# Expert weights in stored blocks of 16 KB per partition, in a ring of ten 16 KB slots and one of 8 KB

## The chip, the cores and the metric

The kernel runs on one core of one Trainium2 chip. The metric is the device time of the program in microseconds (us): three runs of the kernel before took 1932.21, 1930.95 and 1932.10 us, the median is 1932.1 us. All data are f32; weights come from HBM (the chip's main memory) into SBUF (128 partitions of on-chip memory), matrix products go to PSUM.

## What is computed

One layer of a diffusion backbone: a state-space branch and an attention branch over 512 latent tokens, then a routed feed-forward part. The change touches only the last part:

```python
def expert_choice_ffn(h, w_router, w_gate, w_up, w_down):
    cap = CAPACITY_FACTOR * n // N_EXPERTS            # 2 * 512 // 16 = 64 tokens for each of 16 experts
    aff = softmax(h @ w_router)
    gate, idx = top_k(aff.T, cap)
    xs = h[bidx, idx]
    hid = silu(einsum('becd,edf->becf', xs, w_gate)) * einsum('becd,edf->becf', xs, w_up)
    ys = einsum('becf,efd->becd', hid, w_down) * gate[..., None]
    return zeros_like(h).at[bidx, idx].add(ys)
# w_gate, w_up: 16 x 1024 x 2816, w_down: 16 x 2816 x 1024, f32
```

So each of 16 experts reads three matrices of 1024 x 2816 f32, 11 MiB each: 33 MiB an expert, 528 MiB (553.6 MB) in all. Every byte is read once.

## The kernel before

Everything up to about 610 us of the span is the two branches, the output projection and the router; the expert loop follows. `gather(e)` collects the 64 tokens of an expert by a one-hot product (tile `pxg`), transposes them into `xe`. The hidden width of 2816 goes by chunks (`chunks`): five of 512 columns and one of 256. For each chunk `hidden` forms gate and up products side by side in one PSUM tile `pgu` (partitions 0 to 63 gate, 64 to 127 up; k = 0 to 7 runs over the model dimension in the outer loop), then SiLU on ScalarE (ACT), the product on VectorE (DVE), four transposes (`phT`) and a copy `hT`; `down` adds the chunk's share of the down projection into `pdn`. At the end of an expert, `ye` is scattered into the output by an indirect DMA from GpSimd (`out<-ye,sidx`).

The weights are stored by the host (`layout`) in blocks of 128 partitions x 2048 f32: 8 KB per partition, 1 MiB a block. Gate and up are separate arrays; a full chunk takes two blocks of gate (k = 0 to 3, k = 4 to 7), two of up and two of down. Each block is one DMA on SP's queue (line 1444, in `ring`) into one slot of a ring of 21: 13 buffers of the pool `b8r`, 7 of `b8l` and one pair of halves in `hf`, in the order of `RING`. These pools also serve the attention and projection part before (tiles such as `wos`, `mT`, `w_out`), so the first pass round the ring waits for their last readers. A slot comes free when TensorE (PE) has made its last matmul from it.

What sets the order of the work: outside a hand-ordered first part the framework's scheduler orders each engine's instructions by a model of its own. DMAs of SP and ACT take eight semaphores (DMAHW0 to DMAHW7) in turn, and a DMA is not issued before the one eight places ahead on its semaphore has landed: at most eight are under way. ACT issues eight of them itself at this place: the stores `out<-xm` of the residual stream (line 1398, four tiles of two halves), after which `xm` is scaled in place (line 1401) and read by `gather(0)`.

```python
RING = "rrrrlllrrrrrllllrrrrh"
...
w = 2048 // rn
for t, c in ts_:
    dma(t, src[:, c])
    rows_ += [t[:, w * i:w * i + w] for i in range(t.shape[1] // w)]
```

Of the kernel before, what the change touches and what calls it, by code (L numbers as in the profile page):

```python
# [18 lines left out]
D = 1024  # L19
# [7 lines left out]
NE = 16  # L27
CAP = 64
FF = 2816
# [19 lines left out]
NPK = _off  # L49
NTRI = 193  # L50
NR, NL = 13, 7
RING = "rrrrlllrrrrrllllrrrrh"


@with_exitstack
def hybrid_block(ctx: ExitStack, tc: tile.TileContext, A, out, dbg=None, stop=99):
    nc = tc.nc
    V, S, G, T = nc.vector, nc.scalar, nc.gpsimd, nc.tensor
    dma, dmr = nc.sync.dma_start, G.dma_start

    def pool(name, st=ctx, **kw):
        return st.enter_context(tc.tile_pool(name=name, bufs=kw.pop("bufs", 1), reuse_waits="tile", **kw))
# [6 lines left out]
    cur = {}  # L69
# [4 lines left out]
    def tl(p, name, shape, dt=F32):  # L74
        return cur[p].tile(shape, dt, name=name, tag=p)
# [139 lines left out]
    for j in range(4):  # L215
        t = tl("xx", f"X{j}", [NCH, 2, D])
# [416 lines left out]
    for k in range(8):  # L633
# [4 lines left out]
        h = tl("gt", "hxf", [128, 512])  # L638
# [222 lines left out]
    for gb in range(4):  # L861
# [16 lines left out]
        t, y = s5_T(gb, yb)  # L878
# [8 lines left out]
            s5_B(gb + 1)  # L887
            win_prep()
    ph1s.close()
    cur["b8r"] = pool("b8r", bufs=NR, side="right")  # L890

    def b8(name, shape, dt=F32, r="r"):
        return tl("b8" + r, name, shape, dt)
# [69 lines left out]
    t = tl("gt", "krt2", [128, 6, 32])  # L963
# [20 lines left out]

    cur["late"] = pool("late")
    g2bc = cst("g2bc", [128, 512], p="late")
    for n, k in (("l2", 4), ("hf", 2), ("m4", 4), ("b8l", NL)):
        cur[n] = pool(n, bufs=k)


    vt = [b8("vx", [128, 4, 512], r="l"), tl("hf", "vc", [128, 2, 512])]
# [437 lines left out]
    o2 = out.rearrange("t (h d) -> (t h) d", h=2)  # L1429
    chunks = [(512 * i, 512) for i in range(5)] + [(2560, 256)]  # L1430
    nring = [0]

    def ring(name, src, rn):

        r = RING[nring[0] % len(RING)]
        nring[0] += 1
        rows_ = []
        if r == "h":
            ts_ = [(tl("hf", name, [128, 1024]), slice(1024 * i, 1024 * i + 1024)) for i in range(2)]
        else:  # L1440
            ts_ = [(b8(name, [128, 2048], r=r), slice(0, 2048))]
        w = 2048 // rn
        for t, c in ts_:
            dma(t, src[:, c])
            rows_ += [t[:, w * i:w * i + w] for i in range(t.shape[1] // w)]
        return rows_

    def gather(e):

# [31 lines left out]
    nxt_ = gather(0)  # L1481
    for e in range(NE):
        xe, ge, sidx = nxt_
        wg, wu, wd = [A[n][e] for n in ("w_e_gate", "w_e_up", "w_e_down")]
        po = pg("pdn")

        def load_gu(f0, fn):
            r = []
            for w, nm in ((wg, "wg"), (wu, "wu")):
                for i in range(f0 // 256, (f0 + fn) // 256):  # L1490
                    r += ring(nm, w[i], 2048 // fn)
            return r

        def load_d(f0, fn):
            r = []
            for i in range(f0 // 256, (f0 + fn) // 256):
                r += ring("wd", wd[i], 2)
            return r

        def hidden(wt_, fn):  # L1500
            p = pw("pgu", (128, 512))
            for k in range(8):
                for j in range(2):
                    T.matmul(p[64 * j:64 * j + 64, :fn], xe[:, k, :], wt_[8 * j + k], start=(k == 0), stop=(k == 7))  # L1504
            hd = l2("hd", [64, 512])
            S.activation(hd[:, :fn], p[0:64, :fn], AF.Silu)  # L1506
            mul(hd[:, :fn], hd[:, :fn], p[64:128, :fn])
            ph = pa("phT", (128, 4, 64))
            n = fn // 128
            for b in range(n):  # L1510
                T.transpose(ph[:, b, :], hd[:, 128 * b:128 * b + 128], ident[0:64, 0:64])  # L1511
            hT = l2("hT", [128, 4, 64])
            S.copy(hT[:, :n], ph[:, :n])  # L1513
            return hT

        def down(hT, td, f0):
            for b, w in enumerate(td):
                for h in range(2):
                    T.matmul(po[64 * h:64 * h + 64, :], hT[:, b, :], w[:, 512 * h:512 * h + 512],  # L1519
                             start=(f0 == 0 and b == 0), stop=(f0 + 128 * b == FF - 128))  # L1520

        if e < NE - 1:
            for f0, fn in chunks:
                if f0 == 1536:
                    nxt_ = gather(e + 1)
                wt_, td = load_gu(f0, fn), load_d(f0, fn)
                down(hidden(wt_, fn), td, f0)
        else:
            hts = []
            for i, (f0, fn) in enumerate(chunks):  # L1530
                hts.append(hidden(load_gu(f0, fn), fn))
                if i:
                    f1, fm = chunks[i - 1]
                    down(hts[i - 1], load_d(f1, fm), f1)
            down(hts[-1], load_d(f0, fn), f0)
        ye = l2("ye", [128, 512])
        stt(ye, po, ge, g2bc, ALU.mult, ALU.mult)
        G.indirect_dma_start(out=o2, out_offset=bass.IndirectOffsetOnAxis(ap=sidx, axis=0),  # L1538
                             in_=ye, in_offset=None, compute_op=ALU.add)
# [3 lines left out]
def layout(inputs):  # L1543
    import numpy as np

    a = {k: np.asarray(v) for k, v in inputs.items()}
    f32 = np.float32
    pk = np.zeros((128, NPK), f32)

    def put(n, v):  # L1550
        o, w = PK[n]
        pk[:v.shape[0], o:o + w] = v

    def cols(v):
        return np.ascontiguousarray(v.reshape(-1, 128).T)

    def ssm(v):
        rest = v.shape[3:]
        v = v.reshape((2, 4, 2, 4, 64) + rest)
        v = np.moveaxis(v, (2, 4, 1, 0, 3), (0, 1, 2, 3, 4))  # L1560
        return np.ascontiguousarray(v).reshape((128, 32) + rest)

    put("c", cols(a["c"][0]))
    put("cc", cols(a["c_ctx"]))
    put("bada", cols(a["b_ada"][0]))
    put("g1n", cols(a["norm1_g"][0]))
    put("g2n", cols(a["norm2_g"][0]))
    put("qag", cols(a["q_a_g"][0]))
    put("kvag", cols(a["kv_a_g"][0]))
    put("bglu", cols(a["b_glu"][0]))  # L1570
    put("sd", a["ssm_d"][0].reshape(4, 2, 4, 16).transpose(2, 1, 3, 0).reshape(128, 4))
    put("lre", ssm(a["ssm_lam_re"][0]))
    put("lim", ssm(a["ssm_lam_im"][0]))
    put("ldt", ssm(np.broadcast_to(a["ssm_log_dt"][0][:, :, None], (2, 32, 64))))
    put("gq", a["q_norm_g"][0][:, None])
    put("gk", a["k_norm_g"][0][:, None])
    sw = np.arange(32).reshape(2, 2, 8)[:, ::-1].reshape(-1)
    gq, gk = a["q_norm_g"][0][64:], a["k_norm_g"][0][64:]
    put("grope", np.broadcast_to(np.concatenate([gq, gq[sw], gk, gk[sw]]), (128, 128)))
    tok = (8 * np.arange(64)[None, None, :] + 2 * np.arange(4)[:, None, None] + np.arange(2)[None, :, None]).reshape(4, 128)  # L1580
    inv = f32(10000.0) ** (-np.arange(8, dtype=f32) / f32(8))
    pos = np.stack([tok // 64, tok % 64], -1).astype(f32)
    ang = (pos[..., None] * inv).astype(np.float64)
    cs, sn = np.cos(ang), np.sin(ang)
    cs = np.stack([cs, cs], 3).reshape(4, 128, 32)
    sn = np.stack([-sn, sn], 3).reshape(4, 128, 32)
    put("rcos", cs.transpose(1, 0, 2).reshape(128, 128).astype(f32))
    put("rsin", sn.transpose(1, 0, 2).reshape(128, 128).astype(f32))
    put("tok", tok.T.astype(f32))
    put("ident", np.eye(128, dtype=f32))  # L1590
    put("hmask", np.tile(np.eye(16, dtype=f32), (8, 1)))
    put("stack", np.tile(np.eye(32, dtype=f32), (4, 1)))

    def ct(v):
        return ssm(np.swapaxes(v, -1, -2))

    tri = np.zeros((128, NTRI), f32)
    tri[:, :128] = np.triu(np.ones((128, 128), f32))
    tri[:, 128:192] = np.arange(1, 65)
    tri[64:, 192] = 1  # L1600
    r = {"pk": pk, "tri": tri,
         "ssm_b": np.ascontiguousarray(np.stack([ssm(a["ssm_b_re"][0]), ssm(a["ssm_b_im"][0])], 1)),
         "ssm_c": np.ascontiguousarray(np.stack([ct(a["ssm_c_re"][0]), ct(a["ssm_c_im"][0])], 1)),
         "x": a["x"][0], "ctx": a["ctx"][0]}
    for n in ("w_ada", "b_ada", "w_in", "w_qb", "w_kvb", "w_mla_o", "w_glu", "w_ssm_o", "w_out", "w_router"):
        r[n] = a[n][0]

    for n in ("w_e_gate", "w_e_up"):
        w = a[n][0].reshape(NE, 8, 128, FF).transpose(0, 2, 1, 3)
        b = np.empty((NE, 11, 128, 2048), f32)  # L1610
        m = w[..., :2560].reshape(NE, 128, 2, 4, 5, 512).transpose(0, 4, 2, 1, 3, 5)
        b[:, :10] = m.reshape(NE, 10, 128, 2048)
        b[:, 10] = w[..., 2560:].reshape(NE, 128, 2048)
        r[n] = b
    w = a["w_e_down"][0].reshape(NE, 11, 2, 128, D).transpose(0, 1, 3, 2, 4)
    r["w_e_down"] = w.reshape(NE, 11, 128, 2048)
    return {k: np.ascontiguousarray(v) for k, v in r.items()}


# [17 lines left out]
```

## Time and profile before

| | |
|---|---|
| median of 3 runs | 1932.1 us (1930.95 to 1932.21) |
| the profiled execution's own time | 1933.22 us |
| its span, first to last instruction | 1931.4 us |
| mean granted TensorE clock | 0.96 |
| PE busy | 1661.3 us (86%) |
| DVE, ACT, POOL busy | 530.1, 320.6, 209.7 us |
| moved by DMA | 642.61 MB, HBM read 623.93 MB |
| gate loads, 1024 KB each | x176, median 19.9 us from issue to landing |
| stores `out<-xm`, 256 KB each | x8, median 3.1 us |

The page cuts the span into 40 slices of 48.3 us. A digit is the busy share of a slice in tenths; under DMA it is that of the core's 16 DMA engines, under GB/s what they moved. A PE that is busy 86% of the time isn't PE at its peak, since matmuls overlap. Which wait ends last in a stage is read from the chain of waits and from the stage's own windows.

### The profile page before, as it was taken

Reading aid. Unit: us, or ns where it says so; the run is one execution under the profiler, and the core shown is the slowest. Engines: PE = TensorE matmul, PEld = TensorE weight load, DVE = VectorE, ACT = ScalarE, POOL = GpSimd, SP = SyncE. Lnnn points to the kernel's source line nnn. Section 1 sums busy time; section 2 is a strip of 40 time slices with the busy share of each in tenths; the row PEclk is TensorE's granted clock in tenths of the full one; section 3 lists DMA queues with packets and bytes.
Section 4 is the critical chain, followed back from the end, with each engine's and each line's share of the span. In section 5 each row is a group of like instructions: output and inputs, shape, how many; then the busy total and the mean of one; then the engine's idle time right before and its main releaser. Section 6 shows DMA issues by size and latency. Waiting matters only on the chain.

```text
span 1931.4 us, 21472 instructions
## 1 busy us (share of the span) xinstructions
PE 1661.3 (86%) x8660; PEld 806.7 (42%) x8660; DVE 530.1 (27%) x1180; ACT 320.6 (17%) x593; POOL 209.7 (11%) x218
## 2 busy tenths in 40 slices
PE   4798999999996998888888888888888888888887
PEld 2576778755673343323333233333323233332322
DVE  8877655666744100000010010101000010000000
ACT  3422225464421100000000000000000000000000
POOL 3767100231110000000000000000000000000000
PEclk8899999999997999999999999999999999999999
DMA  9253353434675999999999999999999999999997
GB/s 315 64 144 110 109 190 112 169 125 176 170 290 223 419 414 420 414 414 419 414 414 419 414 420 415 419 414 414 420 415 420 414 419 414 414 420 414 420 414 286
DMA packets 149122, 642.61 MB, mean 333 GB/s; under 512 B 14752, under 2 KB 49568, under 8 KB 84128
## 3 DMA queue, kind: packets, MB, share of 16 engines
q1 hardware_dynamic: 145504, 631.81, 82.1%
q0 software_dynamic: 2880, 7.34, 1.7%
q10 hardware_dynamic: 640, 2.10, 0.4%
q8 instruction: 68, 1.11, 0.2%
q14 instruction: 30, 0.25, 0.0%
HBM read 623.93 MB, written 17.27 MB: 332 GB/s over the span
## 4 chain that ended last, share of the span: by engine, by line
PE 45%; DMA 34%; DVE 7%; issue 5%; ACT 3%; POOL 2%; POOLq 0%; SPq 0%; ACTq 0%; DVEq 0%
DMA wu<-in_w_e_up 16%; PE pgu L1504 15%; DMA wg<-in_w_e_gate 9%; DMA wd<-in_w_e_down 8%; PE pdn L1519 8%; PE pxg L1457 2%; PE po L1259 1%; DVE hd L93 1%; PE px L121 1%; PE px L123 1%; PE px L122 1%; ACT hd L1506 1%; PE ada L190 1%; PE phT L1511 1%; PE py L800 1%
## 5 line engine op out<-in xcount | busy, mean ns | idle before, releaser
L1504 PE MATMUL pgu<-wu,xe 128*64 128x512 f32 (+1 forms) x1536 | 630.1, 562 | 31.8 <-DMA wu<-in_w_e_up 31.7
L1504 PE MATMUL pgu<-wg,xe 128*64 128x512 f32 (+1 forms) x1536 | 635.7, 562 | 1.2 <-DVE xe L93 1.2
L1519 PE MATMUL pdn<-wd,hT 128*64 128x512 f32 x1408 | 365.5, 650 | 32.1 <-ACT hT L1513 32.1
L93 DVE TENSOR_TENSOR hd<-hd,pgu 64x512 f32<-64x512 f32 x96 | 62.0, 645 | 1011.4 <-ACT hd L1506 1011.4
L1504 PEld LDWEIGHTS pgu<-wg,xe 128*64 128x64 f32 x1536 | 207.3, 138 | 258.6 <-issue 240.8
L1504 PEld LDWEIGHTS pgu<-wu,xe 128*64 128x64 f32 x1536 | 207.8, 138 | 179.5 <-issue 124.1
L1506 ACT ACTIVATE hd<-pgu 64x512 f32<-64x512 f32 x96 | 53.2, 555 | 967.7 <-PE pgu L1504 967.7
L1519 PEld LDWEIGHTS pdn<-wd,hT 128*64 128x64 f32 x1408 | 114.3, 147 | 215.6 <-issue 164.6
L1538 POOL DMA_INDIRECT out<-ye,sidx x16 | 24.9, 1555 | 1354.9 <-DVE ye L111 1208.4
L1511 PE MATMUL phT<-pk,hd 64*128 64x64 f32 x352 | 42.0, 236 | 118.3 <-DVE hd L93 118.2
L1511 PEld LDWEIGHTS phT<-pk,hd 64*128 64x128 f32 x352 | 28.9, 138 | 195.9 <-DVE hd L93 195.9
L121 PE MATMUL px<-hx,ws 128*128 128x512 f32 x200 | 82.5, 413 | 6.1 <-ACT hx L636 6.1
L122 PE MATMUL px<-hx,ws 128*128 128x512 f32 x200 | 81.0, 405 | 3.3 <-DVE hx L93 3.3
L123 PE MATMUL px<-hx,ws 128*128 128x512 f32 x200 | 80.6, 403 | 1.4 <-DVE ws L93 1.4
L1457 PE MATMUL pxg<-xm,oh 128*64 128x512 f32 x256 | 75.5, 620 | 0.6 <-DVE oh L93 0.6
L1513 ACT COPY hT<-phT 128x256 f32<-128x256 f32 x96 | 34.0, 354 | 119.7 <-PE phT L1511 119.7
L121 PEld LDWEIGHTS px<-hx,ws 128*128 128x128 f32 x200 | 39.1, 195 | 15.3 <-ACT hx L636 6.2
L122 PEld LDWEIGHTS px<-hx,ws 128*128 128x128 f32 x200 | 38.9, 194 | 14.8 <-DVE hx L93 7.5
L123 PEld LDWEIGHTS px<-hx,ws 128*128 128x128 f32 x200 | 38.8, 194 | 10.5 <-DVE ws L93 2.5
L1461 DVE COPY xg<-pxg 128x256 f32<-128x256 f32 x16 | 6.8, 424 | 128.6 <-ACT xg L1460 128.6
L1457 PEld LDWEIGHTS pxg<-xm,oh 128*64 128x64 f32 x256 | 30.1, 142 | 22.9 <-issue 21.3
L1229 DVE TENSOR_REDUCE mx<-ps 128x1 f32<-128x768 f32 x32 | 30.5, 954 | 27.7 <-PE ps L123 25.0
(473 smaller groups left out, 1767.2 us busy)
## 6 DMA issues: line engine op xcount, KB each, us to landing
wg<-in_w_e_gate SPq DMA_DIRECT2D x176, 1024.0 KB, 19.9
wu<-in_w_e_up SPq DMA_DIRECT2D x164, 1024.0 KB, 19.9
wd<-in_w_e_down SPq DMA_DIRECT2D x163, 1024.0 KB, 19.9
wada<-in_w_ada SPq DMA_DIRECT2D x16, 1024.0 KB, 7.3
wd<-in_w_e_down SPq DMA_DIRECT2D x26, 512.0 KB, 18.7
wu<-in_w_e_up SPq DMA_DIRECT2D x24, 512.0 KB, 18.0
wada<-in_w_ada SPq DMA_DIRECT2D x16, 512.0 KB, 10.6
win_g<-in_w_in SPq DMA_DIRECT2D x16, 512.0 KB, 4.2
```

What stands on the lines that cost most here:

```text
L93: (e or V).tensor_tensor(o, a, b, op=op)
L121: T.matmul(o, a[0], b[0], start=first, stop=False)
L122: T.matmul(o, a[0], b[1], start=False, stop=False)
L123: T.matmul(o, a[1], b[0], start=False, stop=last)
L1229: V.tensor_reduce(mx, p[:, 0:768], AX.X, ALU.max, negate=True)
L1457: T.matmul(px[64 * h:64 * h + 64, :], oh[:, t], xms[t][:, 512 * h:512 * h + 512], start=(t == 0), stop=(t == 3))
L1504: T.matmul(p[64 * j:64 * j + 64, :fn], xe[:, k, :], wt_[8 * j + k], start=(k == 0), stop=(k == 7))
L1506: S.activation(hd[:, :fn], p[0:64, :fn], AF.Silu)
L1511: T.transpose(ph[:, b, :], hd[:, 128 * b:128 * b + 128], ident[0:64, 0:64])
L1513: S.copy(hT[:, :n], ph[:, :n])
L1519: T.matmul(po[64 * h:64 * h + 64, :], hT[:, b, :], w[:, 512 * h:512 * h + 512], start=(f0 == 0 and b == 0), stop=(f0 + 128 * b == FF - 128))
L1538: G.indirect_dma_start(out=o2, out_offset=bass.IndirectOffsetOnAxis(ap=sidx, axis=0), in_=ye, in_offset=None, compute_op=ALU.add)
```

## The change

`layout` stores gate and up of one chunk's half (k = 0 to 3, or 4 to 7) side by side as one block of 128 x 4096 f32, 16 KB per partition; for the chunk of 256 columns one block holds all of gate and up. Down goes in blocks of 16 KB per partition too (512 rows), with an own array of 8 KB per partition for the last 256 rows. Each block is one DMA. The ring has ten slots of 16 KB, six on the right (R0 to R5), four on the left (L0 to L3), each a pool of its own, and `small` of 8 KB for the last block of down. The old pools are closed before it (`ph2`), and the new ones lie in the same memory, so that the first use of a slot waits for the last readers of two old tiles. The number of weight loads goes from 528 blocks (553 DMAs, since one slot in 21 took two halves) to 272.

```diff
-RING = "rrrrlllrrrrrllllrrrrh"
+
+RING = ("L0", "R1", "R3", "R5", "R2", "R4", "R0", "L1", "L2", "L3")
...
-    cur["b8r"] = pool("b8r", bufs=NR, side="right")
+    ph2 = ctx.enter_context(ExitStack())
+    cur["b8r"] = pool("b8r", ph2, bufs=NR, side="right")
...
-    for n, k in (("l2", 4), ("hf", 2), ("m4", 4), ("b8l", NL)):
+    for n, k in (("l2", 4), ("m4", 4)):
         cur[n] = pool(n, bufs=k)
+    for n, k in (("b8l", NL), ("hf", 2)):
+        cur[n] = pool(n, ph2, bufs=k)
...
+    ph2.close()
+    for n in ("R0", "R1", "R2", "R3", "R4", "R5", "small"):
+        cur[n] = pool(n, side="right")
+    for n in ("L0", "L1", "L2", "L3"):
+        cur[n] = pool(n)
 
     def ring(name, src, rn):
...
-        w = 2048 // rn
-        for t, c in ts_:
-            dma(t, src[:, c])
-            rows_ += [t[:, w * i:w * i + w] for i in range(t.shape[1] // w)]
-        return rows_
+        w = src.shape[1]
+        r = "small"
+        if w > 2048:
+            r = RING[nring[0] % len(RING)]
+            nring[0] += 1
+        t = tl(r, name, [128, w])
+        dma(t, src)
+        return [t[:, w // rn * i:w // rn * (i + 1)] for i in range(rn)]
...
         def load_gu(f0, fn):
-            r = []
-            for w, nm in ((wg, "wg"), (wu, "wu")):
-                for i in range(f0 // 256, (f0 + fn) // 256):
-                    r += ring(nm, w[i], 2048 // fn)
-            return r
+            if fn == 256:
+                return ring("wgu", wgu[10], 16)
+            a, b = [ring("wgu", wgu[f0 // 256 + i], 8) for i in range(2)]
+            return a[:4] + b[:4] + a[4:] + b[4:]
 
         def load_d(f0, fn):
-            r = []
-            for i in range(f0 // 256, (f0 + fn) // 256):
-                r += ring("wd", wd[i], 2)
-            return r
+            return ring("wd", wds, 2) if fn == 256 else ring("wd", wd[f0 // 512], 4)
```

How it moves instructions. On SP, the first loads of the ring, before (what a row waits for stands in brackets: DMAHW is an earlier DMA of the eight semaphores, PE, Pool and DVE are the last readers of the slot's old tile):

```order
L903 DMA w_out<-in_w_out 128x4x512 [waits DMAHW4_49,PE_49]
L1444 DMA wd<-in_w_e_down 128x2048 [waits DMAHW5_49]
L1444 DMA wd<-in_w_e_down 128x2048 [waits DMAHW6_49,PE_49]
L1444 DMA wg<-in_w_e_gate 128x2048 [waits DMAHW7_49,Pool_49]
L1444 DMA wg<-in_w_e_gate 128x2048 [waits DMAHW0_49,PE_49]
L1444 DMA wu<-in_w_e_up 128x2048 [waits DMAHW1_49,DMASW0_49,DVE_49]
L1444 DMA wu<-in_w_e_up 128x2048 [waits DMAHW2_49,Pool_49]
L1444 DMA wg<-in_w_e_gate 128x2048 [waits DMAHW3_49]
L1444 DMA wg<-in_w_e_gate 128x2048 [waits DMAHW4_49,Pool_49]
```

and with the change:

```order
L905 DMA w_out<-in_w_out 128x4x512 [waits DMAHW4_49,PE_49]
L1450 DMA wgu<-in_w_e_gu 128x4096 [waits DMAHW3_49,PE_49]
L1450 DMA wgu<-in_w_e_gu 128x4096 [waits DMAHW6_49,PE_49,Pool_49]
L1450 DMA wd<-in_w_e_down 128x4096 [waits DMAHW7_49]
L1450 DMA wgu<-in_w_e_gu 128x4096 [waits DMAHW0_49]
L1450 DMA wgu<-in_w_e_gu 128x4096 [waits DMAHW1_49,DMAHW4_49,PE_49,Pool_49]
L1450 DMA wd<-in_w_e_down 128x4096 [waits DMAHW2_49]
L1450 DMA wgu<-in_w_e_gu 128x4096 [waits DMASW1_49,DMASW0_49,DMAHW3_49,DVE_49,PE_49]
L1450 DMA wgu<-in_w_e_gu 128x4096 [waits DMAHW4_49,DVE_49,PE_49]
L1450 DMA wd<-in_w_e_down 128x4096 [waits DMAHW5_49]
L1450 DMA wgu<-in_w_e_gu 128x4096 [waits DMAHW6_49,DVE_49]
```

The turn of the semaphores tells where ACT's stores `out<-xm` stand: before, the eight first loads take DMAHW5 to DMAHW4 right behind `w_out`; with the change the first load takes DMAHW3, so that six of the eight stores (DMAHW5 to DMAHW2) have their turn ahead of it, and loads two to six each wait for one of them to land (DMAHW6, 7, 0, 1, 2); the eighth and ninth wait for the last two (DMAHW4, 5). Up to the first load, and on ACT, DVE and POOL throughout, the instructions stand in the same order in both.

On PE, the first expert's chunk after the gather of the second expert (`pgu` is gate and up, `phT` the transposes of the chunk ahead, `pdn` down; the numbers tell one chunk from the next), before:

```order
L1504 MATMUL pgu_5673<-wg_5661,xe_5406 64x512
L1511 MATMUL phT_5646<-pk_69,hd_5643 128x64 x4
L1504 MATMUL pgu_5673<-wu_5665,xe_5406 64x512
L1504 MATMUL pgu_5673<-wg_5661,xe_5406 64x512
L1519 MATMUL pdn_5428<-wd_5622,hT_5651 64x512 x4
L1519 MATMUL pdn_5428<-wd_5624,hT_5651 64x512 x4
```

and with the change:

```order
L1505 MATMUL pgu_5636<-wgu_5632,xe_5442 64x512 x8
L1512 MATMUL phT_5656<-pk_69,hd_5653 128x64 x4
L1520 MATMUL pdn_5464<-wd_5634,hT_5661 64x512 x8
L1505 MATMUL pgu_5677<-wgu_5671,xe_5442 64x512 x8
```

Before, the scheduler puts the next chunk's first products ahead of this chunk's transposes in the first expert and part of the second, and in plain order in the later ones; with the change the plain order begins at the third chunk of the first expert.

## Rows read from the trace of the kernel before

**Rows 1.** The page, its second part: DMA share and rate in 40 slices.
```profile
DMA  9253353434675999999999999999999999999997
GB/s 315 64 144 110 109 190 112 169 125 176 170 290 223 419 414 420 414 414 419 414 414 419 414 420 415 419 414 414 420 415 420 414 419 414 414 420 414 420 414 286
```

**Rows 2.** Windows: us, busy PE, PEld, DVE, ACT, POOL; PEclk, DMA share, GB/s.
```profile
610.00:620.00 10.00, 8.60 (x40) 3.25 (x39) 1.67 (x8) 0.37 (x1) 0.00 (x0) 0.65 0.11 45
620.00:630.00 10.00, 9.17 (x36) 2.97 (x38) 1.38 (x7) 0.47 (x1) 0.00 (x0) 0.83 0.29 101
...
640.00:740.00 100.00, 94.58 (x482) 38.77 (x478) 11.30 (x35) 8.13 (x19) 1.68 (x1) 1.00 1.01 417
...
1740.00:1840.00 100.00, 83.87 (x416) 31.25 (x412) 7.96 (x21) 6.79 (x15) 1.54 (x1) 0.98 1.02 417
```

**Rows 3.** SP's waits over the whole span: total us, times, longest.
```profile
SPq L1444 <- DMA wg<-in_w_e_gate: 349.0, 164, 3.3
```

**Rows 4.** The chain of waits, in order of time: start us, us, what.
```profile
813.49 6.92 PE pgu L1504 x30
...
892.16 6.92 PE pgu L1504 x30
...
970.90 6.92 PE pgu L1504 x30
...
990.37 17.44 DMA wd<-in_w_e_down
```

**Rows 5.** Timeline of SP's queue, 522 to 640 us: start us, us, instructions.
```profile
522.56 4.96 SPq L1444 DMA_DIRECT2D wd<-in_w_e_down  x2
...
595.35 31.00 SPq L1444 DMA_DIRECT2D wu<-in_w_e_up  x3
626.44 3.34 SPq L1444 DMA_DIRECT2D wd<-in_w_e_down  x2
629.87 3.34 SPq L1444 DMA_DIRECT2D wg<-in_w_e_gate  x2
636.01 2.04 SPq L1444 DMA_DIRECT2D wu<-in_w_e_up  x2
```

**Rows 6.** The end of the timelines of SP's queue and of PE.
```profile
1898.26 5.32 SPq L1444 DMA_DIRECT2D wd<-in_w_e_down  x3
...
1918.60 5.37 PE L1519 MATMUL pdn<-wd,hT 128*64 128x512 f32 x24
```

**Rows 7.** DMA view of 20 to 28 us, rows of 2 KB (`wada`): packets; queue, packets, MB, share.
```profile
DMA packets 1698, 3.27 MB, mean 408 GB/s; under 512 B 103, under 2 KB 103, under 8 KB 1698
...
q1 hardware_dynamic: 1698, 3.27, 105.4%
```

**Rows 8.** DMA view of 640 to 655 us, rows of 8 KB (expert weights).
```profile
DMA packets 869, 6.32 MB, mean 421 GB/s; under 512 B 98, under 2 KB 98, under 8 KB 98
...
q1 hardware_dynamic: 869, 6.32, 101.5%
```

**Rows 9.** Timeline of ACT, 565 to 610 us: the stores and the scaling behind them.
```profile
569.52 0.48 ACTq L1398 DMA_DIRECT2D out<-xm  x1
...
576.60 1.12 ACTq L1398 DMA_DIRECT2D out<-xm  x2
...
583.08 0.47 ACTq L1398 DMA_DIRECT2D out<-xm  x1
...
591.21 1.12 ACTq L1398 DMA_DIRECT2D out<-xm  x2
...
600.98 1.15 ACT L1401 ACTIVATE xm<-xm,inf 128x1024 f32<-128x1024 f32 x1 [6.81 <-DMA out<-xm]
```

**Rows 10.** The chain of waits from 610 us: the first gather, products and down.
```profile
611.27 6.55 PE pxg L1457 x16
...
620.83 12.03 PE pgu L1504 x46
...
655.49 3.43 PE pdn L1519 x16
658.92 3.43 PE pxg L1457 x16
```

More of the change, by code (lines that the diff above doesn't have):

```diff
@@ L1431, in hybrid_block @@
     nring = [0]
-    def ring(name, src, rn):
[L1435 to L1441, printed above, removed]
-        w = 2048 // rn
-        for t, c in ts_:
-            dma(t, src[:, c])
-            rows_ += [t[:, w * i:w * i + w] for i in range(t.shape[1] // w)]
-        return rows_
+    ph2.close()
[3 more added lines that the diff above has]
+        cur[n] = pool(n)
+    def ring(name, src, rn):
+        w = src.shape[1]
[6 more added lines that the diff above has]
+        return [t[:, w // rn * i:w // rn * (i + 1)] for i in range(rn)]
     def gather(e):
@@ L1483, in hybrid_block @@
         xe, ge, sidx = nxt_
-        wg, wu, wd = [A[n][e] for n in ("w_e_gate", "w_e_up", "w_e_down")]
+        wgu, wd, wds = [A[n][e] for n in ("w_e_gu", "w_e_down", "w_e_down_end")]
         po = pg("pdn")
         def load_gu(f0, fn):
-            r = []
-            for w, nm in ((wg, "wg"), (wu, "wu")):
-                for i in range(f0 // 256, (f0 + fn) // 256):
-                    r += ring(nm, w[i], 2048 // fn)
-            return r
+            if fn == 256:
+                return ring("wgu", wgu[10], 16)
+            a, b = [ring("wgu", wgu[f0 // 256 + i], 8) for i in range(2)]
+            return a[:4] + b[:4] + a[4:] + b[4:]
         def load_d(f0, fn):
-            r = []
-            for i in range(f0 // 256, (f0 + fn) // 256):
-                r += ring("wd", wd[i], 2)
-            return r
+            return ring("wd", wds, 2) if fn == 256 else ring("wd", wd[f0 // 512], 4)
         def hidden(wt_, fn):
@@ L1606, in layout @@
         r[n] = a[n][0]
[L1608 to L1616, printed above, removed]
+    w = [a[n][0].reshape(NE, 8, 128, FF).transpose(0, 2, 1, 3) for n in ("w_e_gate", "w_e_up")]
+    b = np.empty((NE, 11, 128, 2, 2048), f32)
+    for i in range(2):
+        m = w[i][..., :2560].reshape(NE, 128, 2, 4, 5, 512).transpose(0, 4, 2, 1, 3, 5)
+        b[:, :10, :, i] = m.reshape(NE, 10, 128, 2048)
+        b[:, 10, :, i] = w[i][..., 2560:].reshape(NE, 128, 2048)
+    r["w_e_gu"] = b.reshape(NE, 11, 128, 4096)
+    w = a["w_e_down"][0]
+    r["w_e_down"] = w[:, :2560].reshape(NE, 5, 4, 128, D).transpose(0, 1, 3, 2, 4).reshape(NE, 5, 128, 4096)
+    r["w_e_down_end"] = w[:, 2560:].reshape(NE, 2, 128, D).transpose(0, 2, 1, 3).reshape(NE, 128, 2048)
     return {k: np.ascontiguousarray(v) for k, v in r.items()}
```

## The prediction

> **What bounds the kernel now.** I read the page's slices first. From the fourteenth slice on (628 us) the DMA engines are busy nine tenths and more in every slice and move 414 to 420 GB/s to within one slice of the end [rows 1]; that is two thirds of the span. The windows say the same without a gap: DMA share 1.01 and 417 GB/s from 640 to 740 us, 1.02 and 417 GB/s from 1740 to 1840 us, while PE is busy 84 to 95% [rows 2]. SP's waits agree: before a load of gate weights it waited 164 times, 349.0 us in all, for an earlier weight load to land, and never longer than 3.3 us [rows 3]; it always has the next load ready when the queue takes it.
>
> The chain of waits names PE from 620 to 990 us and only then DMA. That is not a contradiction. In this stretch PE works off a ring that was filled ahead; experts follow each other at 892.16 - 813.49 = 78.7 us and 970.90 - 892.16 = 78.7 us [rows 4], and each hands free 33 MiB in that time, faster than the DMA engines bring it: 33 MiB = 34.6 MB at 417 GB/s are 83 us. So PE catches up by 4 us an expert, and at 990 us it has caught up. From then on it waits for weights. The end of the kernel is set by the stream of weights: when it starts, what it moves, and the tail behind its last load.
>
> **Start and end of the stream.** The ring's first loads go out at 522.56 us; the third load of the group at 595.35 us cannot go before the first slot is read, and SP stands there for 31.00 us [rows 5]. By 611 us all 21 slots, 21 MiB, are full: the DMA share falls to 0.11, then 0.29 [rows 2]. PE's first weight matmuls start at 620.83 us [rows 10] and free the first slots at 626.44 us [rows 5]; the share of 0.29 over 620 to 630 us puts the restart at 627 to 628, and I take 628. The last three loads are issued from 1898.26 us on, the last about 1903.3; PE ends at 1918.60 + 5.37 = 1923.97 us [rows 6], its last 24 matmuls back to back. The loads take some 18 to 20 us to land, and the last 8 of these matmuls, from about 1922 on, did not wait: I put the end of the stream at 1921. So 528 - 21 = 507 MiB take 1293 us, 2.55 us a MiB, including the 16 scatters. The profiled execution took 1933.22 us for a span of 1931.4; I apply differences to the median, 1932.1, which lies 1.1 us below it.
>
> **Part 1: rows of 16 KB.** A row of a load is one packet. How much of a packet's time is its own and how much its bytes' I take from two stretches in which the queue was full and nothing else ran. Rows of 2 KB: 1698 packets, 103 of them the small completion packets, so 1595 rows in 8 us of 16 engines; rows of 8 KB: 869 - 98 = 771 rows in 15 us [rows 7, 8].
>
> - By progress: 8 x 16 / 1595 = 80.3 ns between rows of 2 KB, 15 x 16 / 771 = 311.3 ns between rows of 8 KB. Per byte that is (311.3 - 80.3) / 6144 = 37.6 ps, and 3.3 ns are left per row. One row of 16 KB in place of two of 8 KB saves 3.3 of 622.6 ns, 0.5%.
> - By the time that packets took (share x time x 16 / rows): 1.054 x 128 / 1595 = 84.6 ns and 1.015 x 240 / 771 = 316.0 ns; 37.7 ps per byte, 7.5 ns per row. The saving is 7.5 of 632 ns, 1.2%.
>
> The two differ because neighbouring packets overlap (shares of 105.4% and 101.5%). I take 0.9%, above the first value since the number of loads halves too, and with it the completion packets, 98 in 15 us in rows 8, which the 2 KB stretch has once in 16 rows and the 8 KB stretch once in 8. On some 1275 us of weights that is -11.5 us; the ends are -6 us and -15 us. No row of 16 KB of such a load is in this trace, so nothing excludes a gain of nothing either.
>
> The Trainium skill, DMA: Bandwidth & Descriptors, section "Why small descriptors are slow (HBM only)", gives a fixed overhead of about 3 cycles per packet beside one cycle per 32 bytes. By it, as an estimate from that page, 259 cycles become 257.5 per 8 KB, 0.6%, or -7.5 us in place of -11.5; the trace's 3.3 to 7.5 ns of 311 to 316 are 1.1 to 2.4% of a packet against the page's 1.2%.
>
> **Part 2: the first filling.** By the order, loads two to six each wait for one of ACT's stores to land, eight and nine for the last two; before, the loads only took turns with them. The stores go out at 569.52, 576.60 (two), 583.08 and about 584, and 591.21 us (two) [rows 9], and land in 3.1 us on the median, longer under load. The first load moves before 545 us. The second starts about 573 us, the third about 581, and from there the queue is not empty: eight loads of 2 MiB at 5.0 us (by rows 8, 2.1 MB at 421 GB/s) are 40 us, and the stores' remaining MB adds about 4: the tenth load lands about 625. That is just when the first slot comes free, since a block's four k steps end where those of two blocks of gate and up ended, at 626. So the idle time of 611 to 628 us vanishes, but it only held what was loaded earlier. At 628 us 20 MiB are there in place of 21 (the 8 KB slot has its turn at the end of an expert): +2.5 us. Behind it the queue is thin once: the first two slots come free at 626.4 and 629.9, the third with the end of `pdn` at about 637.7, some 1.7 us after the queue ran dry. If the filling ends a little late this gap closes. I take +0.5.
>
> **Part 3: coarser pieces and PE's order.** The last load is 1 MiB as before, the one ahead of it 2 MiB: its 16 matmuls (3.43 us, as in row 655.49 of rows 10) can start only when both halves are there, about 1 us before the end of the stream, and the last 8 follow; I take +0.5 us. The number of matmuls doesn't change. The plain order from the first expert's third chunk on costs PE some 10 us in the first two experts, which the chain shows at 78.7 us an expert for the plain order [rows 4]. It is covered by the stream: 620.83 + 16 x 78.7 is 1880, and the stream ends 30 us later. SP issues 272 loads in place of 553, which is hidden anyway.
>
> **Sum.** -11.5 + 2.5 + 0.5 + 0.5 = -8 us: 1924 us. About 0.2% (3.9 us) is what a measurement of this kernel tells from no change.
>
> **Rivals.**
>
> *The saving is larger* (15%): what recurs per load, at the hand-over from one to the next, halves as well. For it speaks that the window of 640 to 655 us moves 421 GB/s [rows 8], while 37.7 ps per byte would be 425; if half of that 0.9% goes too, the saving is 1.7%, -21.5 + 3.5 = -18: 1914 us.
>
> *A row of 16 KB goes no faster than two of 8 KB* (12%), because it is cut into the same packets or the time is all bytes. Against it speaks the step from 408 to 421 GB/s between 2 KB and 8 KB. Then only the costs are left: 1935.6 us, no change by the bound, just.
>
> *The small stores wait behind the big packets* (5%). ACT's last two stores were issued at 591.21 us, and the scaling that waits for them began at 600.98 after 6.81 us of idle time [rows 9], in the midst of loads of 8 KB rows. If they take twice as long with 16 KB rows, the scaling ends at about 611, where the gather starts at 611.27 [rows 10]: no loss. From there each further us delays PE's first matmul and with it the restart of the stream; at three times as long it is 8 us: 1932 us. By the Trainium skill, DMA: Bandwidth & Descriptors, section "Queues, rings and completion order", an engine switches between queues at packet bounds only, which would make the wait per turn about twice as long; the 6.81 us are the row that bears on it.
>
> *Slower: the coarse ring runs dry at the gathers* (8%). From the end of `pdn` at 658.92 PE frees no weights until the next chunk's fourth k step, about 9 us later [rows 10]; the queue must hold two loads (10 us). By then nine big loads and the small one have been freed, 19 MiB or 48 us from 628 us: enough until 675, so 7 us to spare, and with PE gaining 4 us an expert the spare grows. If it is not there (a later first release, PE slower in its plain order), each of the first four gathers costs about 3.5 us, together 14: 1938 us. It decides where fewer than two loads are queued at 659 us.
>
> **Chances and range.** My forecast (1919 to 1929 us) has 60%. Faster by over 0.2% (below 1928.2) are nearly all of it and the larger saving: 70%. Within 0.2% fall most of the unchanged rate, the stores and the upper rim of the forecast: 18%. Slower are the dry ring and an unchanged rate with any further loss: 12%. The range reaches from the larger saving to just short of the unchanged rate: 1914 to 1934 us.
>
> **What would show it.** The DMA rate in slices without a scatter: 420 before, 423 to 425 if right, 420 if the rate is unchanged. One DMA share near 1.0 from 573 to 1900 us but for a dip near 639; a second dip at each gather would be the dry ring. PE's first `pgu` stays at 620.8 us, unless the stores are late. Weights' packets should halve in number. The prediction is wrong if the rate rises and the end doesn't move, or if PE, not DMA, ends the chain in the last experts.

## The result, and the profile after

The changed kernel takes 1918.32 us (median of four runs, 1917.08 to 1919.85) against 1932.15 us for the kernel before beside it: ratio 0.9926 (95% interval 0.9911 to 0.9940), so 13.8 us faster. Measured again later on another occasion (six runs, 1920.43 to 1927.38 us, before 1931.54) it was 1921.74 us, ratio 0.9950, interval 0.9931 to 0.9969, so 9.8 us faster. The forecast was 1924 us, in a range of 1914 to 1934. The profiled execution of after took 1919.85 us, its span 1918.1 us, 13.3 us under the span before.

The page of after, second part (DMA share in tenths and GB/s in 40 slices), beside [rows 1]:

```profile
DMA  9243353525539899999999999999999999999996
GB/s 316 57 141 111 105 189 133 170 97 201 157 90 401 363 422 426 422 427 420 422 427 422 421 426 422 426 423 423 425 421 427 421 427 421 420 428 421 427 422 281
```

Slices without a scatter move 426 to 428 GB/s where they moved 419 and 420, those with one 420 to 423 in place of 414. The forecast for slices without a scatter was 423 to 425. The slices just ahead tell the other side: 90, 401, 363 where there were 290, 223, 419. The first filling comes later and is not over when PE starts.

The same in bytes, from the DMA view of 740 to 1880 us (queue, packets, MB, share of the 16 engines; q1 is the queue of the weights), first before, then after:

```profile
q1 hardware_dynamic: 67596, 470.23, 99.6%
```

```profile
q1 hardware_dynamic: 33864, 478.53, 98.9%
```

Half the packets, and 8.30 MB more in the same 1140 us: 419.8 GB/s of weights in place of 412.5, 1.77%. The prediction's term was 0.9%.

Windows of after (us, busy PE, PEld, DVE, ACT, POOL; granted clock, DMA share, GB/s), beside [rows 2]:

```profile
610.00:620.00 10.00, 5.11 (x19) 3.05 (x21) 4.75 (x11) 0.00 (x0) 0.00 (x0) 0.50 1.00 429
620.00:630.00 10.00, 8.35 (x52) 3.10 (x50) 2.33 (x11) 0.37 (x1) 0.00 (x0) 0.96 0.57 242
630.00:640.00 10.00, 10.00 (x48) 3.37 (x46) 0.69 (x1) 2.25 (x3) 0.00 (x0) 1.00 0.98 387
640.00:650.00 10.00, 9.46 (x48) 3.24 (x46) 0.69 (x1) 0.96 (x2) 0.00 (x0) 1.00 0.90 346
640.00:740.00 100.00, 87.39 (x430) 32.61 (x428) 9.05 (x24) 7.76 (x17) 1.68 (x1) 0.98 1.00 416
```

The idle time of 611 to 628 us is gone, as worked out; what is left of it is the gap of 620 to 630 us. The thin queue that was forecast near 639 us shows as 0.90 and 346 GB/s from 640 to 650. Behind it the share is 1.00 and more: no second dip at the gathers.

SP's queue (timeline: start us, us, instructions), beside [rows 5]:

```profile
533.95 39.98 SPq L1450 DMA_DIRECT2D wgu<-in_w_e_gu  x2
581.85 0.33 SPq L1450 DMA_DIRECT2D wd<-in_w_e_down  x1
582.45 9.60 SPq L1450 DMA_DIRECT2D wgu<-in_w_e_gu  x2
595.11 0.33 SPq L1450 DMA_DIRECT2D wd<-in_w_e_down  x1
595.62 9.31 SPq L1450 DMA_DIRECT2D wgu<-in_w_e_gu  x2
607.65 0.33 SPq L1450 DMA_DIRECT2D wd<-in_w_e_down  x1
608.08 21.67 SPq L1450 DMA_DIRECT2D wgu<-in_w_e_gu  x2
```

One load before 545 us, the second at the end of the first row's 39.98 us, at 573.6, the third at 581.85: these are the prediction's times. Three rows (of 9.60, 9.31 and 21.67 us) hold SP for a store or a slot. The last load of these rows, the first into a slot that was used before, goes out at the end of the 21.67 us, about 629.4, not 626.4: PE starts late. ACT's queue shows why (timeline, the wait ahead of an instruction in brackets), beside [rows 9]:

```profile
583.70 0.47 ACTq L1402 DMA_DIRECT2D out<-xm  x1
584.65 0.47 ACTq L1402 DMA_DIRECT2D out<-xm  x1
588.71 1.14 ACT L1405 ACTIVATE xm<-xm,inf 128x1024 f32<-128x1024 f32 x1
595.20 1.15 ACT L1405 ACTIVATE xm<-xm,inf 128x1024 f32<-128x1024 f32 x1 [5.35 <-DMA out<-xm]
595.29 1.12 ACTq L1402 DMA_DIRECT2D out<-xm  x2
607.74 1.15 ACT L1405 ACTIVATE xm<-xm,inf 128x1024 f32<-128x1024 f32 x1 [7.46 <-DMA out<-xm]
```

The scaling of the third tile waits 5.35 us for its stores of 583.70 and 584.65. Behind it in ACT's queue stand the last tile's stores (595.29, before 591.21) and its part of the router, on which the gather depends. Of PE's delay 0.6 us lie ahead of the change: the third tile's first store goes out at 583.70 us, and at 583.08 before [rows 9]. The chain of waits of after (start us, us, what), beside [rows 4, 10]:

```profile
617.38 5.34 PE pxg L1462 x16
...
625.73 10.51 PE pgu L1505 x46
...
824.53 6.92 PE pgu L1505 x30
...
903.06 6.92 PE pgu L1505 x30
...
1085.93 38.95 DMA wd<-in_w_e_down
```

PE's first gather starts 6.1 us later than before and its first `pgu` 4.9 us later. An expert takes 903.06 - 824.53 = 78.5 us, as before, and PE catches up with the stream at 1086 us, not at 990, since the stream now brings an expert's 34.6 MB in 82 us (at 424 GB/s) and PE gains less per expert. The end of PE, beside [rows 6]:

```profile
1905.11 5.37 PE L1520 MATMUL pdn<-wd,hT 128*64 128x512 f32 x24
```

1910.48 us, 13.5 us ahead of before's 1923.97. In the last experts PE still waits for weights, so the stream still sets the end (PE's groups from 1800 us on: line, operation, tiles; busy us, mean ns; idle before):

```profile
L1505 PE MATMUL pgu<-wgu,xe 128*64 128x512 f32 (+1 forms) x272 | 56.3, 559 | 7.8 <-DMA wgu<-in_w_e_gu 7.8
```

**Where the 13.5 us come from.** From 640 us to its end, queue q1 moved 526.44 MB before and 528.83 MB after: at 640 us after is 2.39 MB behind, 5.7 us at 419.8 GB/s. From 640 to 740 both moved the same (41.36 and 41.31 MB, the faster rows and the thin queue cancel). The 485.1 MB that were left at 740 us before take 485.1/412.5 = 1176.0 us at the old rate and 1155.6 at the new: -20.4 us. With +5.7 and +0.1 that is -14.6. The +1.1 us that are left to the measured -13.5 are a remainder: they lie between the stream's last bytes and PE's end, and were not measured by themselves.

### The profile page after: what moved, and what is told of

It reads as the page before. It is cut to its first block, busy times and chain, and to the rows that moved or that the text cites. A ratio compares the mean times of both kernels' runs of the same rounds, so it can differ in the third digit from the quotient of the medians.

```text
span 1918.1 us, 20921 instructions
## 1 busy us (share of the span) xinstructions
PE 1633.8 (85%) x8660; PEld 791.5 (41%) x8660; DVE 531.5 (28%) x1180; ACT 320.7 (17%) x593; POOL 209.9 (11%) x218
## 4 chain that ended last, share of the span: by engine, by line
PE 43%; DMA 36%; DVE 8%; issue 5%; ACT 3%; POOL 2%; POOLq 0%; ACTq 0%; SPq 0%; DVEq 0%
DMA wgu<-in_w_e_gu 18%; PE pgu L1505 14%; DMA wd<-in_w_e_down 10%; PE pdn L1520 8%; DMA wd<-in_w_e_down_end 6%; PE pxg L1462 2%; PE po L1263 1%; DVE hd L94 1%; PE px L122 1%; PE px L124 1%; PE px L123 1%; ACT hd L1507 1%; PE ada L191 1%; PE phT L1512 1%; PE py L801 1%
## 5 line engine op out<-in xcount | busy, mean ns | idle before, releaser
L1505 PE MATMUL pgu<-wgu,xe 128*64 128x512 f32 (+1 forms) x3072 | 644.9, 559 | 27.5 <-DMA wgu<-in_w_e_gu 26.0
L1505 PEld LDWEIGHTS pgu<-wgu,xe 128*64 128x64 f32 x3072 | 219.9, 137 | 426.5 <-issue 351.1
L1520 PE MATMUL pdn<-wd,hT 128*64 128x512 f32 x1408 | 357.5, 645 | 34.5 <-ACT hT L1514 34.5
L124 PEld LDWEIGHTS px<-hx,ws 128*128 128x128 f32 x200 | 38.2, 191 | 10.2 <-DVE ws L94 2.5
L354 PE MATMUL xT<-pk,X 96*128 96x96 f32 x64 | 11.5, 348 | 29.1 <-DMA craw<-in_ssm_c 18.7
L191 PE MATMUL ada<-wada,scv 128*32 128x512 f32 x192 | 34.1, 675 | 0.0
```

The source lines that it names most:

```text
L124: T.matmul(o, a[1], b[0], start=False, stop=last)
L191: T.matmul(p[32 * q:32 * q + 32, :], scv[:, k].rearrange("p s n -> p (s n)"), w[q], start=(k == 0), stop=(k == 7))
```

## The experiments

Theory R: the packet is what costs; each row of a load has a time of its own, and half the rows save half of it. Theory L: the load is what costs; half the loads have half the hand-overs from one load to the next. Both changed together.

### Rows of 8 KB in the same loads

The changed kernel's ring, loads and order, but each partition of a load is two rows of 8 KB (256 bytes apart in HBM, so that they stay two).

```diff
...
-        dma(t, src)
+        if w > 2048:
+            dma(t.rearrange("p (i n) -> p i n", i=2), src[:, :, 0:2048])
+        else:
+            dma(t, src)
...
```

> The changed kernel with one thing undone: each 16 KB slot is still filled by one load of 2 MiB, but the host stores each partition's block as two rows of 8 KB with 256 bytes between them, so that a row is 8 KB again. Theory R (the gain is the row's: fewer, longer packets): the DMA rate in slices without a scatter falls from 427 GB/s to 420, as before, and the stream becomes 1.7% longer, 21 us: 1939 us; if the stores of the residual stream land sooner between packets of 8 KB, up to 5 us less, 1934. Theory L (the gain comes from half as many loads, their completions and hand-overs): the rate stays at 427 and the time at 1918.

1937.06 us (1935.93 to 1939.87), ratio 1.0028, interval 1.0018 to 1.0038. The DMA view from 740 to 1880 us:

```profile
q1 hardware_dynamic: 61211, 471.13, 99.5%
```

471.13 MB, against 470.23 of before: the rate of the kernel before, to 0.2%, with half its loads. The 256 bytes between the rows cost nothing that shows, since before's rows lie without them. Of the gain of 8.30 MB the longer rows bring 7.40, so theory R holds and L is out. The change without its long rows is slower than no change, by 4.9 us: its costs at the start are left (528.52 MB from 640 us to the end, 2.08 more than before, 5.0 us at 413.3 GB/s). The run also parts the two causes of ACT's wait, below.

### Rows of 4 KB in the same loads

The same with `i=4` and rows of 1024 values.

> As the kernel with rows of 8 KB, but four rows of 4 KB per partition in each load of 2 MiB. Theory R with a fixed price per packet: two packets more per 16 KB cost twice what the step from 16 to 8 KB costs, 3.4% more: 406 GB/s in slices without a scatter, stream 43 us longer than with 8 KB rows, about 1980 us. Theory L: 427 GB/s, 1918 us. If the price is not per packet but belongs to long rows alone, the rate lies between, near 420.

1969.46 us (1967.20 to 1971.27), ratio 1.0192, interval 1.0173 to 1.0210. The page's rate (40 slices) and the DMA view from 740 to 1880 us:

```profile
GB/s 310 67 148 97 119 188 126 138 172 123 220 109 402 400 405 404 411 404 410 404 404 410 406 409 404 409 405 405 409 406 410 404 409 405 405 409 405 410 404 282
```

```profile
q1 hardware_dynamic: 114077, 459.77, 100.8%
```

Slices without a scatter are at 409 to 410 GB/s. In time for 16 KB on one of 16 engines: 16 x 4 x 4096 bytes at 409.5 GB/s are 640.2 ns, two rows of 8 KB at 420 are 624.2, one of 16 KB at 427 is 613.9. Each row saved is worth 8.0 ns from four rows to two and 10.2 ns from two to one, much the same at either length: a reading error of 1 GB/s is 0.8 and 1.4 ns. With one price for every packet, 406 GB/s and about 1980 us were expected; the first step came out a little cheaper than the second. The step of 4 KB to 8 KB alone (8.0 of 624.2 ns, 1.3%) would have forecast the change better than the 0.9% that was taken.

### Two loads per slot: halves, then even and odd partitions

To test L from the other side, the rows of 16 KB stay and the loads are as many as before. First as two halves of 64 neighbouring partitions:

```diff
-        dma(t, src)
+        for i in range(w // 2048):
+            n = 128 * 2048 // w
+            dma(t[n * i:n * i + n], src[n * i:n * i + n])
```

> The changed kernel with twice as many loads at the same row: each 16 KB slot is filled by two loads of 64 partitions, 1 MiB each, rows of 16 KB. Theory R (rows): the rate stays at 427 GB/s and the time within 3 us of 1918. Theory L (number of loads): 420 GB/s, 1939 us.

2735.72 us, ratio 1.4157, interval 1.4113 to 1.4200. Both theories missed by 800 us. The page's rate:

```profile
GB/s 224 118 107 136 155 135 170 170 124 214 216 216 213 223 217 225 218 220 221 221 228 229 236 234 254 362 323 331 369 276 296 268 272 297 286 324 277 326 315 189
```

For 15 slices, some 1000 us, the stream runs at 213 to 236 GB/s, half of 427, with the DMA engines marked busy throughout. So the edit brought in a limit of its own and tells nothing of L. Is it the 64 rows, or that they are neighbours? The second version takes every other partition:

```diff
-        dma(t, src)
+        for i in range(w // 2048):
+            n = w // 2048
+            dma(t[i:128:n], src[i:128:n])
```

> The changed kernel, but each slot of 16 KB per partition is filled by two loads of 1 MiB, one for the even and one for the odd partitions, both with rows of 16 KB (the run with two halves of 64 neighbouring partitions moved only about 220 GB/s). So the rows are those of the changed kernel and the number of loads that of the kernel before. If the slowness of the halves came from writing to 64 neighbouring partitions at a time, these loads, spread over all partitions, run at full rate: then theory R (rows alone) gives 427 GB/s in slices without a scatter and 1917 to 1920 us, theory L (what recurs per load) 420 GB/s and about 1937 us. If it came from loads of only 64 rows, it is slow again: 216 to 280 GB/s, about 2700 us, and R against L stays with the run of 8 KB rows.

1922.57 us (1918.46 to 1925.01), ratio 0.9949, interval 0.9932 to 0.9966; the changed kernel beside it took 1921.74. From 740 to 1880 us:

```profile
q1 hardware_dynamic: 37380, 478.18, 99.0%
```

478.18 MB, to 0.1% the changed kernel's 478.53, with 1 MiB loads. L is refuted twice, and the loss of the halves came from filling 64 neighbouring partitions at a time. The Trainium skill, SBUF — State Buffer, section "Door 1: The DMA port swizzle", says that partitions 0 to 63 and 64 to 127 lie on different halves of the 16 ports through which DMA writes; the two runs agree with it (half the rate in one, all of it in the other). Why the halves later in the run reach 270 to 370 GB/s is open.

### Without the in-place scaling

Theory S, called Q further on: the late start of PE comes from the third tile's scaling, which waits for its stores. How long do stores take? The third tile's two stores, from the DMA view of 582 to 588 us (queue, count, KB each, median us from issue to landing), in the kernel before, in after, with rows of 8 KB and with rows of 4 KB:

```profile
out<-xm ACTq DMA_DIRECT2D x2, 256.0 KB, 3.0
```

```profile
out<-xm ACTq DMA_DIRECT2D x2, 256.0 KB, 9.0
```

```profile
out<-xm ACTq DMA_DIRECT2D x2, 256.0 KB, 7.6
```

```profile
out<-xm ACTq DMA_DIRECT2D x2, 256.0 KB, 7.5
```

Before, the ring's loads went out from 585.10 us on, behind these stores; with the change two loads of 2 MiB go out at 581.85 and 582.45, just ahead of them. In the run with rows of 32 KB at the end of this section the loads go out behind the stores again, from 584.51 us on, and the median is 3.0 us again. The medians hide one thing: the scaling waits for the later of the two stores. ACT's third scaling before (two in one row, no wait ahead of them), with rows of 8 KB and with rows of 4 KB, beside after's 595.20 with a wait of 5.35 us:

```profile
588.07 2.17 ACT L1401 ACTIVATE xm<-xm,inf 128x1024 f32<-128x1024 f32 x2
```

```profile
592.24 1.15 ACT L1405 ACTIVATE xm<-xm,inf 128x1024 f32<-128x1024 f32 x1 [2.96 <-DMA out<-xm]
```

```profile
591.84 1.15 ACT L1405 ACTIVATE xm<-xm,inf 128x1024 f32<-128x1024 f32 x1 [2.67 <-DMA out<-xm]
```

So of the 5.35 us about half, 2.7 to 3.0, comes from loads ahead of the stores, with rows of 4 and of 8 KB alike, and 2.4 more come with rows of 16 KB. To see what the wait costs, the scaling was left out, so that the experts get unscaled tokens:

```diff
-    for t in range(4):
-        S.activation(xms[t], xms[t], AF.Copy, scale=inf[:, t, 1:2])
```

> The changed kernel without the scaling of xm in place (ACT's four activations behind the router are left out, so that the experts get unscaled tokens). Nothing then waits for the stores of the residual stream but their semaphores. Theory S (the stores land late between the big packets, ACT waits for them at the third tile and holds up the last tile's router): PE's first weight matmul moves from 625.7 us back to about 620.8, and the end with it, 1913.5 us. Theory F (the filling of the ten slots, over at 627 us, sets the restart): the first matmul moves but the end stays within 1 us of 1918.

1917.22 us, ratio 0.9916, interval 0.9892 to 0.9939, but the four runs lie in two pairs: 1913.77 and 1914.24 us at mean clocks of 0.966 and 0.968, 1920.20 and 1920.57 at 0.946 and 0.945. The profiled execution is one at 0.946. Its first `pgu` starts at 623.56 us, 2.2 earlier than in after where 4.9 were expected, since the part ahead of the change ran late in it: the third tile's first store went out at 586.54 us. From there to the first `pgu` it is 37.0 us, against 42.0 in after and 37.8 before, so the wait is gone. And yet the span is no shorter. PE's groups from 1800 us on:

```profile
L1503 PE MATMUL pgu<-wgu,xe 128*64 128x512 f32 (+1 forms) x288 | 57.6, 545 | 0.0
```

In after the same group has 7.8 us of idle time behind `wgu`, here none: PE doesn't wait for weights any more, and ends the kernel itself. Its experts by the chain of waits:

```profile
744.67 6.92 PE pgu L1503 x30
...
823.26 6.92 PE pgu L1503 x30
...
905.22 6.92 PE pgu L1503 x30
```

They follow each other at 78.6 us first, as in after, and at 82.0 us from 823 us on, which is what the stream takes for an expert. The granted clock is seen in the windows of the stage, first of this run, then of after:

```profile
1240.00:1840.00 600.00, 521.25 (x2471) 191.37 (x2471) 52.72 (x143) 43.01 (x96) 10.82 (x7) 0.93 1.01 424
```

```profile
1240.00:1840.00 600.00, 503.83 (x2468) 183.91 (x2468) 53.45 (x144) 43.04 (x96) 12.38 (x8) 0.97 1.01 424
```

The time is lost in the down products: from 640 us on a `pdn` takes 704 ns in the mean in this run, 645 in after. So the faster stream has nearly used up PE's spare time. Of the two expectations S was right for the start; between an end 5 us earlier (S) and the same end (F) these runs don't decide: two end 4 us before 1918, two end 2 us behind it. Whether the pairs repeat was asked of the next version.

### The scaling moved behind the gather

The per-token factor is gathered with the indices, ahead of the tokens, and the two copies out of PSUM multiply by it.

```diff
-    for t in range(4):
-        S.activation(xms[t], xms[t], AF.Copy, scale=inf[:, t, 1:2])
...
+        rs = sm("rsg", [128, 1])
+        V.tensor_copy(rs, pi[:, 1:2])
...
-        S.copy(xg[:, 0:256], px[:, 0:256])
-        V.tensor_copy(xg[:, 256:512], px[:, 256:512])
+        S.activation(xg[:, 0:256], px[:, 0:256], AF.Copy, scale=rs)
+        ts(xg[:, 256:512], px[:, 256:512], rs)
```

> The changed kernel, but the in-place scaling of xm on ScalarE is gone: the per-token factor is gathered with the indices (its small products now stand ahead of the gather's), and the two copies of the gathered tokens multiply by it. The output is that of the reference. Theory Q (the third tile's scaling, which waits for its store behind 16 KB packets, holds ScalarE's queue and delays PE's first product): without it the first pgu starts 2 to 4.5 us earlier than the changed kernel's 625.7, at 621 to 623.5 us, and the stream of weights ends 2 to 4 us earlier. Theory Q1 (the stream alone sets the end): 1914 to 1916 us. Theory Q2 (PE is nearly as long as the stream, and its granted clock decides the last experts): about 1914 at a mean clock of 0.965 and above, about 1920 at 0.945, so a median between these by chance of the clock. Rival N (the start costs nothing): first pgu and time as in the changed kernel.

> The changed kernel once more, on the chip of the run without the scaling, for a comparison side by side. Expected 1917 to 1920 us. If PE's clock decides the end (Q2), executions at a mean granted clock below 0.95 are 2 us or more longer than those above 0.96; if the stream alone does (Q1), the times don't go with the clock.

1916.51 us (six runs, 1911.63 to 1918.45; ratio 0.9916, interval 0.9897 to 0.9934) against 1921.74 us (1920.43 to 1927.38) of the changed kernel beside it: 5.2 us less, and the two sets don't overlap (against the changed kernel's first four runs, median 1918.32, it is 1.8 us less). On another occasion it took 1915.60 us (four runs, 1914.05 to 1916.98; ratio 0.9916, interval 0.9891 to 0.9940):

> The version without the in-place scaling once more, beside the run with rows of 32 KB: 1914 to 1918 us.

The chain of waits and the end of PE in the first of these:

```profile
623.36 10.51 PE pgu L1505 x46
...
1324.96 40.34 DMA wgu<-in_w_e_gu
```

```profile
1901.94 5.37 PE L1520 MATMUL pdn<-wd,hT 128*64 128x512 f32 x24
```

and the changed kernel's beside it:

```profile
628.30 10.51 PE pgu L1505 x46
```

```profile
1907.04 5.37 PE L1520 MATMUL pdn<-wd,hT 128*64 128x512 f32 x24
```

PE starts 4.9 us earlier and ends 5.1 us earlier: theory Q holds, N (the start costs nothing) is refuted. Not all of it is the wait, since the part ahead of the change varies from run to run: the third tile's first store goes out at 583.70 and 585.68 us in the two profiles of the changed kernel, at 584.57 and 582.96 in those of this version. From there PE's first `pgu` comes after 42.0 and 42.6 us in the changed kernel, after 38.8 and 37.6 in this version and after 37.8 before, so the wait is worth some 4 us.

What counts at the end is not PE's start but the bytes that the stream has left. From 740 us on these are 488.67 MB in the changed kernel and 486.51 here: 2.16 MB, 5.1 us at 419.8 GB/s. In the run with even and odd partitions PE's first `pgu` came at 621.23 us, 7.1 us earlier than in the changed kernel beside it. But the first filling was thin there (DMA share 0.91 and 0.93 from 590 to 610 us), 488.17 MB were left at 740 us, and PE ended at 1911.83 us, beside 1912.41.

Q2, the clock, stays half open: all ten runs of this version had clocks of 0.963 to 0.967, so the lower clock didn't come up, and of the changed kernel's two runs near 0.945 one was no longer than the rest (1920.57 us at 0.947), the other 6 us longer (1927.38 at 0.943). Where the stream sets the end by more, with rows of 8 KB, the clock made no difference: three runs at 0.943 to 0.949 took 1935.93 to 1939.62 us, the six others at 0.957 to 0.966 took 1936.51 to 1939.87.

### Rows of 32 KB

If each row costs some 10 ns whatever its length, gate and up of a chunk in one load with rows of 32 KB should gain again. On the version above, with three slots of 32 KB for them in the same memory:

```diff
-    for n in ("R0", "R1", "R2", "R3", "R4", "R5", "small"):
+    for n in ("G0", "G1", "G2", "small"):
...
-            a, b = [ring("wgu", wgu[f0 // 256 + i], 8) for i in range(2)]
+            a = ring("wgu", wgu[f0 // 512], 16)
+            a, b = a[:8], a[8:]
```

> The version without the in-place scaling (factor in the copies), and gate and up of a full chunk in one load of 4 MiB with rows of 32 KB, in three slots of 32 KB; down in three slots of 16 KB, the chunk of 256 columns in one of 16 KB, the rest of down in one of 8 KB, so the same memory. Theory R carried on (each packet has about 10 ns of its own, whatever its length): rows of 32 KB, 20 of 33 MiB an expert, save 10 of 1228 ns, 0.8% there and 0.5% of the stream: slices without a scatter at 427 for gate and up near 430, the mean of 640 to 1880 us 423 to 425, the stream 6 us shorter, and 1909 to 1913 us against about 1916.5. Rival K (a row of 32 KB is cut into two packets of 16 KB): as many packets as with 16 KB and no gain, about 1916 us. Rival S (three slots of 32 KB are too coarse: a slot comes free only with its sixteenth product, and the queue runs dry at the gathers, or the first filling ends early): DMA shares below 0.95 somewhere behind 650 us and a longer time, 1920 to 1940 us.

1920.15 us (1916.26 to 1923.44), ratio 0.9936, interval 0.9915 to 0.9958: 4.5 us slower in the median than the version it is built on (1915.60 beside it, 1914.05 to 1916.98; the two sets just overlap). The DMA view of 640 to 1880 us, of the rows of 32 KB, then of that version:

```profile
q1 hardware_dynamic: 26098, 523.56, 98.8%
```

```profile
q1 hardware_dynamic: 36835, 520.73, 98.9%
```

The stream did what R says: a row of 32 KB stays one packet (10,700 fewer), and the rate rose by 0.54%, 0.5% expected. That is 6.7 us in 1240. They are lost at the first filling. SP's queue:

```profile
584.51 0.35 SPq L1453 DMA_DIRECT2D wgu<-in_w_e_gu  x1
```

This is the first expert load of the program, 52 us after the other version's first (532.11), since a slot of 32 KB lies over the memory of more old tiles: SP waits 52.3 us for PE's `pxm`, the output projection. From 640 us to the end it had 531.21 MB to bring, the other 527.50: 3.71 MB, 8.7 us at 425 GB/s. The two make +2.0 us of the 3.2 between the profiled spans (1916.1 and 1912.9); the rest is not accounted for. Rival K is out; rival S was right in the sign, by the first filling, not by dips at the gathers (DMA share 0.99 and more from 650 us on). A ring that mixes a first load of 16 KB slots with longer rows was not tried.

## Why the prediction was right, and where its terms were off

The mechanism was right: the stream of weights sets the end, longer rows raise its rate, the start gives something back, and PE's order and SP's issues cost nothing. The sum, -8 us, came out as -13.5 at PE's end and -13.8 in the medians. Two of its terms were too small, one on each side, so that the misses partly cancel by luck: 8.9 us too little was saved and 3.4 us too little was lost.

- **What bounds the kernel**: right, shown by rows of 8 and of 4 KB, where the time followed the rate (+18.7 and +51.1 us over after), and still so after the change. But the cover of PE got thin: "the stream ends 30 us later" holds at a clock of 0.965 (625.73 + 16 x 78.5 = 1881.7 us), not near 0.945, where PE took 82.0 us an expert from 823 us on and ended the kernel in one profile.
- **Part 1, the term of -11.5 us**: this is the mis-sized one. It measured -20.4 us (1.77% in place of 0.9%). The step that failed is the own time of a row, 3.3 to 7.5 ns, taken from 8 us of rows of 2 KB and 15 us of rows of 8 KB; measured over the whole stage it is 8.0 ns from 4 to 8 KB rows and 10.2 from 8 to 16 KB. Even the upper end, -15 us, fell short: by the steady rows (4 KB 160.0 ns, 8 KB 312.1, so 37.1 ps per byte) a row of 2 KB would take 84.0 ns, and that early stretch showed 80.3. Why it went faster is not shown.
- The Trainium skill's 3 cycles per packet (DMA: Bandwidth & Descriptors, "Why small descriptors are slow (HBM only)") gave, as an estimate, -7.5 us. The runs differ: 10.2 ns beside 312 ns for a row of 8 KB is 3.3% where 3 of 259 cycles are 1.2%.
- **The rival of the larger saving** gave the rate almost exactly (1.7%) for a wrong reason: it laid the second half on the hand-over between loads. Loads of half the number with the old rows gained 0.2%, and loads of the old number with the new rows lost 0.1%.
- **Part 2, +2.5 and +0.5 us**: the times of the filling and the thin queue near 639 us are in the profile, but the deficit is 5.7 us at 640 us. What failed is that the first slot would come free at 626.4 us: PE started 4.9 us late, and the first load into a used slot went out at 629.4.
- **The rival of the small stores** did happen, at another place. The prediction priced the last tile's scaling, where 9 us of slack were left before the gather. The wait that counted was the third tile's, on the same engine's queue, ahead of the last tile's router work, and the prediction put that at nothing without a reason. About half of it came from loads that now stand ahead of the stores (2.7 and 3.0 us with rows of 4 and 8 KB), the other half from rows of 16 KB (5.35 us with them). By the Trainium skill, DMA: Bandwidth & Descriptors, section "Queues, rings and completion order", an engine switches queues at packet bounds. The trace bears that out only in part: rows of 16 KB add 2.4 us over rows of 8 KB, but rows of 8 KB add only 0.3 over rows of 4 KB.
- **Part 3, +0.5 us**: the remainder that falls to the tail is +1.1; no run tells more of it.
- **The slower rival**, a ring run dry at the gathers, did not happen: the DMA share is 1.00 from 640 to 740 us with the one dip in it.
- "The prediction is wrong if PE, not DMA, ends the chain in the last experts": in after the stream ends it, with 7.8 us of waits left in the last 120 us.

## What to carry to other kernels

Where DMA engines are busy all the time, count packets, not loads: a row cost its bytes and some 8 to 10 ns here, and the price is best read from two row lengths measured over a long steady stretch. Larger pieces move the first filling, though: follow each engine's queue through it, since a store that lands later holds not only its own reader but all that stands behind that reader. After a gain on the bound, work out how much spare the next resource has left, at the lowest clock that was granted.

## What was not expected of the hardware

- Loads to 64 neighbouring partitions ran at some 220 GB/s for 1000 us, loads to 64 of 128 taken alternately at the full 427.
- The own time of a packet depends little on its length: 8.0 ns (4 to 8 KB), 10.2 ns (8 to 16 KB), and a row of 32 KB is still one packet.
- 256 KB stores took 3.0 us to land with nothing ahead of them and 7.5 to 9.0 us behind two loads of 2 MiB on another queue (medians of two stores).
- The mean granted clock of one kernel was 0.945 in some runs and 0.966 in others; in the kernel without the scaling, where PE and the stream were nearly even, the time went with it by 6 us; with rows of 8 KB it did not.
